# Gated linear attention inside a hybrid decoder block: the scores of two 64-token chunks as one 128x128 product, with the decay referred to the boundary between them

## The chip, the cores and the metric

The kernel runs on one NeuronCore of a Trainium2 chip. Its time is the device time of one launch, in microseconds (us): the median of several timed runs. A profiled execution, taken separately, gives the span from the first to the last instruction and the start and duration of every instruction. The engines are called by the profile's names: PE is TensorE's matmul, PEld its weight load, DVE VectorE, ACT ScalarE, POOL GpSimd, SP the engine that issues most DMAs. A matmul holds one operand still in the array (the stationary one, loaded by PEld) and streams the other past it (the moving one).

## The reference

One decoder block on 512 tokens of width 1024, all in float32: a normalized input goes through one wide projection; a gated linear attention (GLA, 4 heads, key width 128, value width 256) and a sparse attention work on its parts; their merged outputs and then a SwiGLU feed-forward are added to the residual. The change touches only the GLA. Cut to what matters (per head; `b` is the running sum of the log decay within a chunk of 64 tokens, `n` counts the 8 chunks):

```
log_a  = log_sigmoid(a_lr @ w_alpha2 + b_alpha) / 16
b      = cumsum(log_a within a chunk);  b_last = b at the chunk's last token
qe     = q * 128**-0.5 * exp(b)
ke     = k * exp(-b)
kd     = k * exp(b_last - b)
attn   = where(causal, qe @ ke.T, 0)              # inside each chunk, 64x64
o      = attn @ v + qe @ state_before_chunk
state  = exp(b_last) * state + kd.T @ v           # from chunk to chunk
```

`o` is then normalized per head and gated.

## The kernel before, in words

**Layout.** Activations are kept transposed: a tile of [128, 512] has 128 features on the partitions and the 512 tokens along the free dimension. For the GLA a head's queries `gq[h]`, keys `gk[h]` and decay sums `lam[:, h]` are such tiles (128 = the key width). The values `tok[n]` have tokens on the partitions, four tiles of 128 tokens. The kernel handles two chunks of 64 at a time, so a head has NT = 4 *pairs*, and the state is carried from pair to pair. Inside a pair the left chunk is s = 0, the right one s = 1; the helper `par` picks one side of all four pairs, a [128, 4, 64] view, 256 columns.

**Dense products.** Each of the many projections (`dense_h` with `prod`, L175 to L196) multiplies a [128 x 1024] weight block with the [1024 x 512] input. Full fp32 accuracy comes from splitting weights and input into a high and a low half in a faster format and adding three products per 128 rows (L182, L183, L184), 24 matmuls with 512 moving columns per block. The class `Stream` brings the weight blocks in: SP's DMA into `wraw` (L53, three buffers), ScalarE's conversion to `whi` (L59, two buffers), VectorE's difference `wlo` (L65, two buffers). It works one block ahead of need. `proj` (L295) evicts a finished block from PSUM with VectorE, times the token's norm factor `rb_x` (L298), or with one more scalar (L300, so far used for the sparse attention's queries).

**Order of the work.** `weave` (L78) puts a list of side steps between the dense blocks. After the blocks of gates, keys and queries, the steps of the four GLA heads are woven into the rest of the list `with_gla` (L546): for each head `gla_prep` (decay factors and products on VectorE, ScalarE and GpSimd), `gla_attn` (scores), `gla_state`, `gla_out`, `gla_end` (gate, and the split into halves at L199 and L200). The order of the steps is preparation 0, scores 0, preparation 1, state 0, output 0, scores 1, preparation 2, end 0, state 1, and so on: a head is prepared right behind the scores of the head before it. The framework adds all semaphores and orders the instructions by its own priorities; `issue_after` keeps a scan of `gla_prep` (L361) behind a given eviction, which `out_of` remembers. Each engine then works its queue in order.

**`gla_prep` (L359 to L397).** From the running sums `lam` it makes: `dd` = last minus running sum (VectorE, L371), `e1` = exp(+b) (ScalarE, L372), `e2` = exp(-b) (L373, one buffer), `dd` exponentiated in place (L374), `el` = exp(last) (L375), `dec` = the decay over a pair (L377). Then the operands. VectorE writes two blocks of `q3` [128, 4, 3, 64]: left queries times exp(b) in block 0, right queries likewise in block 2, both times the scale QSCALE (L387). GpSimd makes six products of [128 x 256]: block 1 of `q3`, the right queries carried over the left chunk (L389); `ke`, the left keys times exp(-b) (L391); `kx`, one side the right keys times exp(-b) (L392), the other the left keys times exp(last - b) (L393); `ku`, the keys for the state (L394, L395).

**`gla_attn` (L399 to L416).** For each of the four pairs two fp32 products into one PSUM bank: `ke` (64 columns, stationary) with block 0 of `q3` gives the left chunk's 64x64 scores (L404); `kx` (128 columns, stationary) with block 2 gives the scores of the right chunk's 64 queries against all 128 keys (L405). Eight masked copies on VectorE take the part on and above the diagonal into `at`, which was zeroed once (L409, L410). Three transposes of `ku` follow (L414) and ScalarE copies them out (L415). `gla_state` multiplies them with the values (L423), and `gla_out` adds the score product (L439) and, from the second pair on, blocks 0 and 1 of `q3` times the state (L441).

After the heads, the space of their tiles is used by the sparse attention, whose compression weights come by a GpSimd DMA (L583) and are read at L609.

Of the kernel before, what the change touches and what calls it, by code (L numbers as in the profile page):

```python
# [8 lines left out]
F32 = mybir.dt.float32  # L9
F32R = mybir.dt.float32r  # L10
U8 = mybir.dt.uint8
AF = mybir.ActivationFunctionType
OP = mybir.AluOpType
# [3 lines left out]
S = 512  # L17
D = 1024
KD = D // 128
NT = S // 128  # L20
# [8 lines left out]
QSCALE = 128.0 ** -0.5  # L29
# [63 lines left out]
def hybrid_block_kernel(ctx: ExitStack, tc: tile.TileContext, I, outT):  # L93
    nc = tc.nc
    act, dve, pool, pe = nc.scalar, nc.vector, nc.gpsimd, nc.tensor
# [35 lines left out]
    rb_x = base.tile([128, S], F32, name="rb_x")  # L131
# [23 lines left out]
    for key in with_gla + with_cmp + with_att + late:  # L155
        kind, n = key
# [72 lines left out]
    for k in range(KD):  # L229
        xt = xin.tile([128, S], F32, tag="xt", bufs=8, name="xt")  # L230
        nc.sync.dma_start(xt, I["xT"][k])
        if k % 2 == 0:
# [3 lines left out]
                                 in1=hT[:, k, :].bitcast(F32), op0=OP.mult, op1=OP.subtract)  # L236
# [12 lines left out]
    for g in range(3):  # L249
        pss = [bank(t) for t in tags[g]]  # L250
        for c in range(4):
            wh, wl = st.next(("tok", g, c))
            for i in range(NT):
                if (g, c, i) == (0, 3, 2):
                    ps = token_sums([acc_x], "acc")
                    rsqrt_mean(rs_x, ps[:, 0:NT], D, EPS)
                t = slice(i * 128, (i + 1) * 128)
# [7 lines left out]
        if g == 0:  # L265
            ps = over_partitions(rs_x, "acc")
# [28 lines left out]
    def proj(n, dst, scale=None):  # L295
        ps = dense_h(n)
        if scale is None:
            out_of[n] = dve.tensor_tensor(out=dst, in0=ps, in1=rb_x, op=OP.mult)  # L298
        else:
            dve.scalar_tensor_tensor(out=dst, in0=ps, scalar=scale, in1=rb_x, op0=OP.mult, op1=OP.mult)  # L300


    p_gt = tc.tile_pool(name="glat", bufs=1, reuse_waits="tile")
# [53 lines left out]
    gst = {}  # L357

    def gla_prep(h):  # L359
        with tc.issue_after(out_of[T_GK + h + 1 if h + 1 < HG else T_GQ + h].ins):  # L360
            dve.tensor_tensor_scan(out=lam[:, h], data0=keep.rearrange("p c t -> p (c t)"), data1=lam[:, h],  # L361
                                   initial=0.0, op0=OP.mult, op1=OP.add)
        bb = lam[:, h].rearrange("p (c t) -> p c t", t=64)
        last = bb[:, :, 63:64]
        T = 1.0 / 16.0
        e1 = gt.tile([128, S], F32, tag="e1", bufs=1, name="e1")
        e2 = gt.tile([128, S], F32, tag="e2", bufs=1, name="e2")
        dd = gt.tile([128, 8, 64], F32, tag="dd", bufs=2, name="dd")
        el = gt.tile([128, 8], F32, tag="el", bufs=2, name="el")
        dec = gt.tile([128, 4], F32, tag="dec", bufs=2, name="dec")  # L370
        dve.tensor_tensor(out=dd, in0=last.to_broadcast([128, 8, 64]), in1=bb, op=OP.subtract)  # L371
        act.activation(out=e1, in_=lam[:, h], func=AF.Exp, scale=T)  # L372
        act.activation(out=e2, in_=lam[:, h], func=AF.Exp, scale=-T)  # L373
        act.activation(out=dd, in_=dd, func=AF.Exp, scale=T)  # L374
        act.activation(out=el, in_=last.rearrange("p c o -> p (c o)"), func=AF.Exp, scale=T)  # L375
        el2 = el.rearrange("p (n two) -> p n two", two=2)
        dve.tensor_tensor(out=dec, in0=el2[:, :, 0], in1=el2[:, :, 1], op=OP.mult)  # L377

        def par(t, s):
            return t.rearrange("p (n two t) -> p n two t", two=2, t=64)[:, :, s, :]  # L380
        ddf = dd.rearrange("p c t -> p (c t)")
        q3 = gt.tile([128, NT, 3, 64], F32, tag="gq3", bufs=2, name="gq3")
        ke = gt.tile([128, NT, 64], F32, tag="gke", bufs=1, name="gke")
        kx = gt.tile([128, NT, 2, 64], F32, tag="gkx", bufs=1, name="gkx")
        ku = gt.tile([128, NT, 2, 64], F32, tag="gku", bufs=1, name="gku")
        for s in range(2):
            dve.scalar_tensor_tensor(out=q3[:, :, 2 * s, :], in0=par(gq[h], s), scalar=QSCALE, in1=par(e1, s),  # L387
                                     op0=OP.mult, op1=OP.mult)
        pool.tensor_tensor(out=q3[:, :, 1, :], in0=q3[:, :, 2, :],  # L389
                           in1=el2[:, :, 0:1].to_broadcast([128, NT, 64]), op=OP.mult)  # L390
        pool.tensor_tensor(out=ke, in0=par(gk[h], 0), in1=par(e2, 0), op=OP.mult)  # L391
        pool.tensor_tensor(out=kx[:, :, 1, :], in0=par(gk[h], 1), in1=par(e2, 1), op=OP.mult)  # L392
        pool.tensor_tensor(out=kx[:, :, 0, :], in0=par(gk[h], 0), in1=par(ddf, 0), op=OP.mult)  # L393
        pool.tensor_tensor(out=ku[:, :, 1, :], in0=par(gk[h], 1), in1=par(ddf, 1), op=OP.mult)  # L394
        pool.tensor_tensor(out=ku[:, :, 0, :], in0=kx[:, :, 0, :],  # L395
                           in1=el2[:, :, 1:2].to_broadcast([128, NT, 64]), op=OP.mult)
        gst[h] = [q3, ke, kx, ku, dec]  # L397

    def gla_attn(h):  # L399
        q3, ke, kx, ku, dec = gst[h]  # L400
        at = ats[h % 2]
        ps = bank("tp")
        for n in range(NT):
            pe.matmul(ps[0:64, n * 128:n * 128 + 64], ke[:, n, :], q3[:, n, 0, :], start=True, stop=True)  # L404
            pe.matmul(ps[:, n * 128 + 64:(n + 1) * 128], kx[:, n].rearrange("p s t -> p (s t)"), q3[:, n, 2, :],  # L405
                      start=True, stop=True)
        p4 = ps.rearrange("p (n c) -> p n c", c=128)
        for n in range(NT):
            dve.copy_predicated(out=at[0:64, n, 0:64], mask=triu8[0:64, 0:64], data=p4[0:64, n, 0:64])  # L409
            dve.copy_predicated(out=at[:, n, 64:128], mask=triu8[:, 64:128], data=p4[:, n, 64:128])  # L410
        ps = bank("tp")
        kut = gt.tile([128, 3, 128], F32, tag="gkut", bufs=1, name="gkut")
        for n in range(3):
            pe.transpose(ps[:, n * 128:(n + 1) * 128], ku[:, n].rearrange("p s t -> p (s t)"), ident)  # L414
        act.copy(kut.rearrange("p n d -> p (n d)"), ps[:, 0:384])  # L415
        gst[h].append(kut)  # L416

    def gla_state(h):
        q3, ke, kx, ku, dec, kut = gst[h]
        ss = gt.tile([128, 3, 256], F32, tag="gs", bufs=2, name="gs")  # L420
        for n in range(3):
            ps = bank("sc")
            pe.matmul(ps[:, 0:256], kut[:, n, :], tok[n][:, h * 256:(h + 1) * 256], start=True, stop=True)  # L423
            if n == 0:
                act.copy(ss[:, 0, :], ps[:, 0:256])
            else:
                dve.scalar_tensor_tensor(out=ss[:, n, :], in0=ss[:, n - 1, :], scalar=dec[:, n:n + 1],
                                         in1=ps[:, 0:256], op0=OP.mult, op1=OP.add)
        gst[h].append(ss)

    def gla_out(h):
        q3, ke, kx, ku, dec, kut, ss = gst[h]
        at = ats[h % 2]
        ps = [bank("acc"), bank("acc")]
        ssq = gt.tile([128, NT], F32, tag="gssq", bufs=2, name="gssq")
        o = gt.tile([128, NT, 256], F32, tag="go", bufs=1, name="go")
        for n in range(NT):
            out = ps[n // 2][:, (n % 2) * 256:(n % 2) * 256 + 256]
            pe.matmul(out, at[:, n, :], tok[n][:, h * 256:(h + 1) * 256], start=True, stop=(n == 0))  # L439
            if n > 0:  # L440
                pe.matmul(out, q3[:, n, 0:2, :].rearrange("p s t -> p (s t)"), ss[:, n - 1, :], start=False, stop=True)  # L441
            act.activation(out=o[:, n, :], in_=out, func=AF.Square, accum_out=ssq[:, n:n + 1])
        rs = gt.tile([128, NT], F32, tag="grs", bufs=2, name="grs")
        rsqrt_mean(rs, ssq, 256, EPS)
        for n in range(NT):
            out = ps[n // 2][:, (n % 2) * 256:(n % 2) * 256 + 256]
            act.activation(out=o[:, n, :], in_=out, func=AF.Copy, scale=rs[:, n:n + 1])
        gst[h] = o
# [58 lines left out]
    def run(key, ps=None):  # L507
        kind, n = key
        if kind == "pa":
            if ps is None:  # L510
                ps = bank("mm")
                prod(ps, st.next(key), lambda k: ah[:, k, :], lambda k: al[:, k, :], 0, 8, 8)
            dve.scalar_tensor_tensor(out=ta[n], in0=ta[n], scalar=1.0, in1=ps, op0=OP.add, op1=OP.mult)
        elif n >= T_MB:
            where = mid2 if n < T_MB + 4 else mixp if n < T_MB + 7 else mix2
            tb[n - T_MB] = merge_gate(n, where.tile([128, S], F32, name="tb%d" % (n - T_MB)), ps)
        elif n >= T_MA:
            ta[n - T_MA] = merge_gate(n, slot(n - T_MA), ps)
        elif n >= T_R:
            proj_r(n - T_R)  # L520
        elif n >= T_KV + 2:
            proj(n, kst["sw"[n - T_KV - 2]])
        elif n >= T_KV:
            compress_in(n)
        elif n >= T_NQ:
            proj(n, qst[n - T_NQ], 0.125)
        elif n >= T_GK:
            proj(n, gk[n - T_GK])
        else:
            proj(n, gq[n])  # L530

    def runs(keys):
        return [lambda key=key: run(key) for key in keys]
# [1095 lines left out]
```

## Time and profile before

| | |
|---|---|
| timed runs | 871.92, 872.35, 873.64 us; median 872.35 |
| profiled execution, its own time as the page gives it (the span) | 870.5 us |
| granted TensorE clock, mean over the span | 0.996 |
| instructions | 13817 |
| score products of a head (8 products, 16 passes) | 2.40 us from the first to the transposes behind them |
| scores of the four heads start at | 112.43, 142.38, 178.85, 215.34 us |
| masked copies | 16 of 64x64, median 216 ns; 16 of 128x64, median 214 ns |

The page lists for each engine the busy time and its share of the span, then the chain of work that ended last, followed back from the last instruction. The trace behind it answers by line, by wait, by stretch of time and as a timeline. In a timeline a row is start, duration, engine, line, operation, the tile written and those read, the shape, and in brackets how long the engine stood idle before it and what released it. Matmul rows show the stationary tile (rows*columns) and then the moving one (partitions x columns). Matmuls are pipelined and their ends are modelled, so what one costs in a stream is the distance between starts. An fp32 matmul appears as two passes, each with its weight load.

### The profile page before, as it was taken

The page shows a single profiled execution, that of the slowest core. Times are in us where ns is not written, and L with a number is a line of the kernel's source. Part 1 is how long each engine was busy: PE and PEld are TensorE (multiplying, and loading weights), DVE is VectorE, ACT ScalarE, POOL GpSimd, SP SyncE. Part 2 cuts the span into 40 slices and gives each one's busy share as a digit, 9 for nine tenths or more (in the row PEclk, how much of TensorE's full clock was granted, in tenths as well). Part 3 has the DMA queues.
Part 4 walks back from the last instruction along what each step waited for, and adds up shares of the span by engine and source line. Part 5 has one row for each costly group of instructions (what it writes and reads, how often), then busy time and mean ns, then how long its engine had stood idle before and what let it go on. Part 6 is the DMA issues. An engine that isn't in the chain of part 4 may idle for free.

```text
span 870.5 us, 13817 instructions
## 1 busy us (share of the span) xinstructions
PE 856.8 (98%) x5268; PEld 759.8 (87%) x5268; DVE 594.5 (68%) x1125; ACT 486.3 (56%) x862; POOL 141.5 (16%) x169
## 2 busy tenths in 40 slices
PE   9999999999999999999999999999999999999995
PEld 8998877887888788888887999899999999889995
DVE  8224753534464888887767468998778779829876
ACT  7335434333362788888744577765666656525441
POOL 1000322020030001000000354111111110001343
PEclk9999999999999999999999999999999999999998
DMA  7332221222241444545317849679877873335222
GB/s 237 97 98 93 97 83 63 79 66 74 73 152 49 120 98 103 117 98 122 85 49 226 269 137 247 125 199 233 186 171 176 195 176 85 94 87 170 86 98 98
DMA packets 36914, 111.23 MB, mean 128 GB/s; under 512 B 4236, under 2 KB 6300, under 8 KB 36720
## 3 DMA queue, kind: packets, MB, share of 16 engines
q1 hardware_dynamic: 27232, 82.49, 29.7%
q0 software_dynamic: 8896, 27.32, 16.8%
q8 instruction: 41, 0.67, 0.3%
q10 hardware_dynamic: 720, 0.54, 0.2%
q14 instruction: 25, 0.20, 0.1%
HBM read 95.66 MB, written 4.19 MB: 115 GB/s over the span
## 4 chain that ended last, share of the span: by engine, by line
PE 91%; ACT 4%; DVE 2%; issue 1%; DMA 1%; POOL 0%; SPq 0%; ACTq 0%; DVEq 0%; POOLq 0%
PE ps_mm L182 11%; PE ps_mm L184 11%; PE ps_mm L183 11%; PE ps_mm L1191 6%; PE ps_tp L1191 6%; PE ps_sc L1191 5%; PE ps_acc L1191 5%; PE ps_sc L1482 4%; PE ps_acc L1482 2%; PE ps_mm L1482 2%; PE ps_tp L792 2%; PE ps_acc L184 1%; PE ps_acc L183 1%; PE ps_acc L182 1%; PE ps_sc L182 1%; PE ps_sc L184 1%
## 5 line engine op out<-in xcount | busy, mean ns | idle before, releaser
L59 ACT CAST whi<-wraw 128x1024 fp32r<-128x1024 f32 (+2 forms) x81 | 80.1, 989 | 150.4 <-PE ps_mm L183 66.9
L182 PE MATMUL ps_mm<-hT_hi,whi 128*128 128x512 f32 x344 | 139.9, 407 | 0.0
L184 PE MATMUL ps_mm<-hT_hi,wlo 128*128 128x512 f32 x344 | 137.0, 398 | 0.0
L183 PE MATMUL ps_mm<-hT_lo,whi 128*128 128x512 f32 x344 | 136.1, 395 | 0.0
L65 DVE TENSOR_TENSOR wlo<-wraw,whi 128x1024 fp32r<-128x1024 f32 (+2 forms) x66 | 75.0, 1137 | 51.1 <-ACT whi L59 51.0
L184 PEld LDWEIGHTS ps_mm<-hT_hi,wlo 128*128 128x128 f32 x344 | 64.7, 188 | 15.4 <-DVE wlo L65 0.3
L182 PEld LDWEIGHTS ps_mm<-hT_hi,whi 128*128 128x128 f32 x344 | 64.9, 189 | 14.0
L183 PEld LDWEIGHTS ps_mm<-hT_lo,whi 128*128 128x128 f32 x344 | 64.9, 189 | 13.0
L752 ACT ACTIVATE p<-p,mx 128x512 f32<-128x512 f32 (+1 forms) x64 | 35.9, 561 | 8.8 <-DVE mx L750 7.8
L200 DVE TENSOR_TENSOR pl<-ps_tp,ph 128x512 fp32r<-128x512 f32 (+1 forms) x64 | 31.0, 489 | 13.2 <-ACT ph L199 12.5
L63 POOL DMA_DIRECT2D wlo<-wraw x15 | 13.0, 864 | 154.2 <-ACT wlo L62 154.2
L750 DVE CUSTOM_DVE_ANT_0 p<-ps_sc,causal 128x512 f32<-128x512 f32 (+1 forms) x64 | 30.2, 486 | 6.2 <-PE ps_sc L743 6.1
L1090 POOL DMA_DIRECT2D w_uu<-in_w_up x19 | 16.4, 865 | 84.6 <-PE ps_sc L1191 27.0
L199 ACT CAST ph<-ps_tp 128x512 fp32r<-128x512 f32 (+1 forms) x64 | 26.3, 415 | 4.1 <-PE ps_tp L792 3.6
L792 PE MATMUL ps_tp<-ident,p 128*128 128x128 f32 x160 | 27.7, 273 | 0.4 <-ACT pc L686 0.3
L792 PEld LDWEIGHTS ps_tp<-ident,p 128*128 128x128 f32 x160 | 20.6, 140 | 8.0 <-ACT pc L686 0.7
L182 PE MATMUL ps_mm<-gla_hi,whi 128*128 128x512 f32 x64 | 26.2, 410 | 0.0
L466 DVE TENSOR_TENSOR sr<-ps_mm,rb_x 128x512 f32<-128x512 f32 x8 | 5.5, 692 | 29.0 <-PE ps_mm L184 29.0
L184 PE MATMUL ps_mm<-gla_hi,wlo 128*128 128x512 f32 x64 | 25.3, 395 | 0.0
L183 PE MATMUL ps_mm<-gla_lo,whi 128*128 128x512 f32 x64 | 25.3, 395 | 0.0
L1106 ACT CAST w_hl<-s 128x1024 fp32r<-128x1024 f32 x12 | 12.6, 1047 | 19.6 <-issue 15.8
L1106 ACT CAST w_d1h<-s 128x1024 fp32r<-128x1024 f32 x13 | 13.7, 1051 | 17.2 <-issue 12.5
(862 smaller groups left out, 2778.2 us busy)
## 6 DMA issues: line engine op xcount, KB each, us to landing
wraw<-in_w_t SPq DMA_DIRECT2D x40, 512.0 KB, 3.5
wraw<-in_w_gate SPq DMA_DIRECT2D x21, 512.0 KB, 5.8
rw<-in_w_up SPq DMA_DIRECT2D x19, 512.0 KB, 4.2
wlo<-wraw POOLq DMA_DIRECT2D x15, 512.0 KB, 4.5
wlo<-in_w_gate POOLq DMA_DIRECT2D x13, 512.0 KB, 7.2
wraw<-in_w_tok SPq DMA_DIRECT2D x12, 440.0 KB, 4.1
w_uu<-in_w_up POOLq DMA_DIRECT2D x19, 256.0 KB, 5.8
wraw<-in_w_proj SPq DMA_DIRECT2D x8, 512.0 KB, 3.5
```

The source lines that it names most:

```text
L59: self.nc.scalar.copy(hi[:, :cols], raw[:, :cols])
L65: self.nc.vector.tensor_tensor(out=lo[:, :cols], in0=raw[:, :cols], in1=hi[:, :cols].bitcast(F32), op=OP.subtract)
L182: pe.matmul(ps[:, t], wh[:, c], xh(k)[:, t], start=(k == 0), stop=False)
L183: pe.matmul(ps[:, t], wh[:, c], xl(k)[:, t], start=False, stop=False)
L184: marks.append(pe.matmul(ps[:, t], wl[:, c], xh(k)[:, t], start=False, stop=(k == ktot - 1)))
L199: act.copy(hi, src)
L200: dve.tensor_tensor(out=lo, in0=src, in1=hi.bitcast(F32), op=OP.subtract)
L750: dve.tensor_tensor_reduce(out=o, in0=s, in1=causal[:, S - n:S], scale=-1.0, scalar=-NEG, op0=OP.add, op1=OP.min, accum_out=mx[:, i:i + 1])
L752: act.activation(out=o, in_=o, func=AF.Exp, scale=-1.0, bias=mx[:, i:i + 1], accum_out=z[:, i:i + 1])
L792: pe.transpose(tp[:, i * 128:(i + 1) * 128], p[:, OFF[i] + k * 128:OFF[i] + (k + 1) * 128], ident)
L1191: pe.matmul(o, w[:, c], x[q], start=(first and q == 0 and i == 0), stop=(q == 3 and i == 2), skip_group_check=True)
L1482: pe.matmul(o, w[:, c], x[q], start=(first and q == 0 and i == 0), stop=(q == KH - 1 and i == 2), skip_group_check=True)
```

## The change

The left queries for the scores are referred to the end of the left chunk: a new block of the query tile holds q * exp(b - last), made from a second factor, exp(-(last - b)). With the left keys in `kx`, which already carry exp(last - b), their product is exp(b_q - b_k), as before. So one stationary tile `kx` (left and right keys, 128 columns) and one moving tile (left and right queries, 128 columns) give all the scores of a pair; the quarter of right keys against left queries is masked out. `ke` goes. The query tile has four blocks now (left with exp(b), right carried over the left chunk, left referred to the boundary, right with exp(b)). `e2` is made by two exponentials, its left half from `dd` before `dd` is exponentiated, its right half from the running sums. The eight masked copies become one over the whole bank. The scale QSCALE moves from `gla_prep` to the eviction of the query projection.

```diff
-            dve.scalar_tensor_tensor(out=dst, in0=ps, scalar=scale, in1=rb_x, op0=OP.mult, op1=OP.mult)
+            out_of[n] = dve.scalar_tensor_tensor(out=dst, in0=ps, scalar=scale, in1=rb_x, op0=OP.mult,
+                                                 op1=OP.mult)
...
-        e2 = gt.tile([128, S], F32, tag="e2", bufs=1, name="e2")
+        e2 = gt.tile([128, NT, 2, 64], F32, tag="e2", bufs=1, name="e2")
...
-        act.activation(out=e2, in_=lam[:, h], func=AF.Exp, scale=-T)
+        b2 = lam[:, h].rearrange("p (n two t) -> p n two t", two=2, t=64)
+        d2 = dd.rearrange("p (n two) t -> p n two t", two=2)
+        act.activation(out=e2[:, :, 0, :], in_=d2[:, :, 0, :], func=AF.Exp, scale=-T)
+        act.activation(out=e2[:, :, 1, :], in_=b2[:, :, 1, :], func=AF.Exp, scale=-T)
...
-        q3 = gt.tile([128, NT, 3, 64], F32, tag="gq3", bufs=2, name="gq3")
-        ke = gt.tile([128, NT, 64], F32, tag="gke", bufs=1, name="gke")
+        q4 = gt.tile([128, NT, 4, 64], F32, tag="gq4", bufs=2, name="gq4")
...
-            dve.scalar_tensor_tensor(out=q3[:, :, 2 * s, :], in0=par(gq[h], s), scalar=QSCALE, in1=par(e1, s),
-                                     op0=OP.mult, op1=OP.mult)
-        pool.tensor_tensor(out=q3[:, :, 1, :], in0=q3[:, :, 2, :],
+            dve.tensor_tensor(out=q4[:, :, 3 * s, :], in0=par(gq[h], s), in1=par(e1, s), op=OP.mult)
+        pool.tensor_tensor(out=q4[:, :, 1, :], in0=q4[:, :, 3, :],
                            in1=el2[:, :, 0:1].to_broadcast([128, NT, 64]), op=OP.mult)
-        pool.tensor_tensor(out=ke, in0=par(gk[h], 0), in1=par(e2, 0), op=OP.mult)
-        pool.tensor_tensor(out=kx[:, :, 1, :], in0=par(gk[h], 1), in1=par(e2, 1), op=OP.mult)
+        pool.tensor_tensor(out=q4[:, :, 2, :], in0=par(gq[h], 0), in1=e2[:, :, 0, :], op=OP.mult)
+        pool.tensor_tensor(out=kx[:, :, 1, :], in0=par(gk[h], 1), in1=e2[:, :, 1, :], op=OP.mult)
...
         for n in range(NT):
-            pe.matmul(ps[0:64, n * 128:n * 128 + 64], ke[:, n, :], q3[:, n, 0, :], start=True, stop=True)
-            pe.matmul(ps[:, n * 128 + 64:(n + 1) * 128], kx[:, n].rearrange("p s t -> p (s t)"), q3[:, n, 2, :],
-                      start=True, stop=True)
+            pe.matmul(ps[:, n * 128:(n + 1) * 128], kx[:, n].rearrange("p s t -> p (s t)"),
+                      q4[:, n, 2:4, :].rearrange("p s t -> p (s t)"), start=True, stop=True)
         p4 = ps.rearrange("p (n c) -> p n c", c=128)
-        for n in range(NT):
-            dve.copy_predicated(out=at[0:64, n, 0:64], mask=triu8[0:64, 0:64], data=p4[0:64, n, 0:64])
-            dve.copy_predicated(out=at[:, n, 64:128], mask=triu8[:, 64:128], data=p4[:, n, 64:128])
+        dve.copy_predicated(out=at, mask=triu8.unsqueeze(1).to_broadcast([128, NT, 128]), data=p4)
...
-                pe.matmul(out, q3[:, n, 0:2, :].rearrange("p s t -> p (s t)"), ss[:, n - 1, :], start=False, stop=True)
+                pe.matmul(out, q4[:, n, 0:2, :].rearrange("p s t -> p (s t)"), ss[:, n - 1, :], start=False, stop=True)
...
-            proj(n, gq[n])
+            proj(n, gq[n], QSCALE)
```

The remaining lines of the diff only rename `q3` to `q4` where the tiles are handed on, and drop `ke` there.

More of the change, by code (lines that the diff above doesn't have):

```diff
@@ L396, in gla_prep @@
                            in1=el2[:, :, 1:2].to_broadcast([128, NT, 64]), op=OP.mult)
-        gst[h] = [q3, ke, kx, ku, dec]
+        gst[h] = [q4, kx, ku, dec]
     def gla_attn(h):
-        q3, ke, kx, ku, dec = gst[h]
+        q4, kx, ku, dec = gst[h]
         at = ats[h % 2]
@@ L418, in gla_state @@
     def gla_state(h):
-        q3, ke, kx, ku, dec, kut = gst[h]
+        q4, kx, ku, dec, kut = gst[h]
         ss = gt.tile([128, 3, 256], F32, tag="gs", bufs=2, name="gs")
@@ L431, in gla_out @@
     def gla_out(h):
-        q3, ke, kx, ku, dec, kut, ss = gst[h]
+        q4, kx, ku, dec, kut, ss = gst[h]
         at = ats[h % 2]
```

## The prediction, on record before the changed kernel ran

> **What bounds the kernel now.** I read the page first: the span, TensorE's busy line and the shares of the chain of work that ended last.
>
> ```profile
> span 870.5 us, 13817 instructions
> PE   856.8 (98%) x5268; PEld 759.8 (87%) x5268; DVE 594.5 (68%) x1125; ACT 486.3 (56%) x862; POOL 141.5 (16%) x169
> PE 91%; ACT 4%; DVE 2%; issue 1%; DMA 1%; POOL 0%; SPq 0%; ACTq 0%; DVEq 0%; POOLq 0%
> ```
>
> TensorE is busy nearly all the time and carries 91% of the chain. An average says nothing about one stage, so next I read the busy time by stretches: from just before the first head's preparation to the last head's end (84 to 250), and the two stretches behind it.
>
> ```profile
> core 0: us, PE busy (x) PEld busy (x) DVE busy (x) ACT busy (x) POOL busy (x), PEclk, DMA share, GB/s
> 84.00:250.00 166.00, 165.92 (x756) 132.47 (x755) 83.34 (x140) 66.28 (x123) 26.89 (x33) 1.00 0.24 77
> 250.00:292.00 42.00, 41.94 (x201) 34.85 (x200) 28.44 (x61) 17.74 (x36) 5.75 (x9) 1.00 0.30 95
> 292.00:362.00 70.00, 69.45 (x373) 56.52 (x372) 58.69 (x171) 61.11 (x137) 6.01 (x7) 1.00 0.48 111
> ```
>
> In the stretch that the change touches, TensorE runs 165.92 of 166 us at the full granted clock; VectorE is busy half of it, ScalarE 40%, GpSimd 16%, the DMA engines 24%. What TensorE does less there, the end should come earlier by, unless another wait takes the place. The waits of this stretch show what the others wait for:
>
> ```profile
> ACT whi L59 <- PE ps_mm L183: 47.8, 16, 5.7
> ...
> POOL gke L391 <- PE ps_tp L404: 22.0, 3, 11.4
> ...
> PEld ps_tp L404 <- issue: 1.5, 4, 0.4
> ...
> ACT e L373 <- POOL gkx L392: 0.7, 2, 0.4
> ```
>
> The weight conversion on ScalarE (L59) stood waiting for TensorE 47.8 us in all: weights are ready ahead of need. The one wait of TensorE's weight loads that belongs to the changed lines is 1.5 us over four heads, ahead of the first score product, and no engine's work ends it.
>
> **The score products, the term that counts.** TensorE around the scores of the first head, from its timeline (start, duration, line; x2 since each fp32 product is two passes):
>
> ```profile
> 112.10 0.40 PE L184 MATMUL ps_mm<-hT_hi,wlo 128*128 128x512 f32 x1
> 112.43 0.33 PE L404 MATMUL ps_tp<-gq,gke 128*64 128x64 f32 x2
> 112.69 0.43 PE L405 MATMUL ps_tp<-gq,gkx 128*128 128x64 f32 x2
> 113.05 0.33 PE L404 MATMUL ps_tp<-gq,gke 128*64 128x64 f32 x2
> ...
> 114.56 0.43 PE L405 MATMUL ps_tp<-gq,gkx 128*128 128x64 f32 x2
> 114.83 0.50 PE L414 MATMUL ps_tp<-ident,gku 128*128 128x128 f32 x3
> ...
> 215.34 0.33 PE L404 MATMUL ps_tp<-gq,gke 128*64 128x64 f32 x2
> ...
> 217.74 0.50 PE L414 MATMUL ps_tp<-ident,gku 128*128 128x128 f32 x3
> ```
>
> Ends of matmuls are modelled, so I count from start to start. A product of L404 takes 0.26 us, one of L405 0.36, the pair of them 0.62 per chunk pair; from the first of the eight to the transposes behind them are 2.40 us, in the last head (215.34 to 217.74) as in the first. From the last dense matmul (112.10) to the transposes (114.83) are 2.73 us.
>
> The new form, a 128-column stationary tile and 128 moving columns in fp32, is in the trace elsewhere, unbroken: the broadcast of the norm's factor (L220). Two neighbours bound it: the same stationary size with 64 moving columns (L659) and with 256 (L423).
>
> ```profile
> 26.83 1.05 PE L220 MATMUL ps_acc<-ident,rs_x 128*128 128x128 f32 x8
> L220 PE MATMUL ps_acc<-ident,rs_x x8: 272/276/276, 26.8 to 27.6; 128*128 128x128 f32 x8
> 274.80 3.79 PE L659 MATMUL ps_sc<-kdg,qst 128*128 128x64 f32 x32
> 126.13 0.39 PE L184 MATMUL ps_mm<-hT_hi,wlo 128*128 128x512 f32 x1
> 126.36 1.03 PE L423 MATMUL ps_sc<-tok,gkut 128*128 128x256 f32 x4
> L423 PE MATMUL ps_sc<-tok,gkut 128*128 128x256 f32 x4 | 1.0, 380 | 0.0
> ```
>
> L220: eight passes from first start to last end in 1.05, one lasting 0.276, so (1.05 - 0.276) / 7 = 0.111 us from start to start. L659: (3.79 - 0.276) / 31 = 0.113, with half the moving columns (its own pass is taken as L220's). So up to 128 moving columns a pass costs the same, 0.111. L423: (1.03 - 0.38) / 3 = 0.217 for 256 columns. A new product is then two passes, 0.223, and four of them 0.89 us. The entry from the dense stream into such a form costs nothing extra: 126.13 to 126.36 is 0.23, the dense matmuls' own spacing, while 112.10 to 112.43 is 0.33. New length from the dense matmul to the transposes: 0.23 + 0.89 = 1.12, or 1.17 if the step to the transposes keeps 0.05 of its present excess (114.56 + 0.11 for the second pass, then 114.83). Saved per head 2.73 - 1.12 = 1.61, or 1.56; for four heads 6.4 or 6.2; I take 6.3. Bounds from the neighbours: a pass can't well be cheaper than the 0.111 that L220 and L659 share, and if it cost the 0.217 of the 256-column row, a head would need 0.23 + 8 x 0.217 = 1.97, saving 0.76, 3.1 in all.
>
> Why the old pair costs 0.62 where two uniform fp32 products cost 0.45: it alternates a 64-column stationary tile with a 128-column one, and each turn costs. The Trainium skill, "TensorEngine Tiling (Array Packing)", Key Properties, says that changing the tiling mode drains the engine; the 0.26 and 0.36 against 0.22 agree with that, but no row here separates it. The forecast doesn't hang on the reason: the old cost is measured whole.
>
> **The rest of TensorE and what is moved.** Transposes (L414), state and output products keep number and form; L441 reads the first two blocks of the new tile as it did of the old.
>
> **VectorE.** Eight masked copies per head become one of 128x512 with the mask repeated.
>
> ```profile
> 115.03 0.22 DVE L409 COPY_PREDICATED at<-triu,ps_tp 64x64 f32<-64x64 uint8 x1 [0.67 <-PE ps_tp L405]
> ...
> 115.96 0.21 DVE L410 COPY_PREDICATED at<-triu,ps_tp 128x64 f32<-128x64 uint8 x1
> 116.09 1.20 DVE L65 TENSOR_TENSOR wlo<-wraw,whi 128x1024 fp32r<-128x1024 f32 x1
> 112.54 0.69 DVE L298 TENSOR_TENSOR gq<-ps_mm,rb_x 128x512 f32<-128x512 f32 x1 [2.06 <-PE ps_mm L184]
> L300 DVE SCALAR_TENSOR_TENSOR qst<-ps_mm,rb_x x4: 691/692/692, 126.6 to 170.0; 128x512 f32<-128x512 f32 x4
> ```
>
> The eight take 115.03 to 116.09, 1.06 us. The trace has no masked copy of that size; the nearest is L298, 128x512 out of PSUM, 0.69; bounds 0.21 (one narrow copy) and 1.06 (no cheaper than now). Gain 0.4 per head on an engine that is idle half the stretch: off the path. What stands queued behind it is the weights' low half (L65), which then comes earlier. The query projections get their scale inside the eviction: L298 (0.69) becomes the form of L300 (0.69), nothing; the two multiplications of 128x256 lose a scalar, nothing that matters.
>
> **ScalarE and GpSimd.** One exponential of 128x512 becomes two of 128x256, the first of which reads the difference tile before that is exponentiated in place. GpSimd's six products per head stay six: the one for the left keys goes, one for the left queries comes, of the same size.
>
> ```profile
> 112.35 1.04 ACT L59 CAST whi<-wraw 128x1024 fp32r<-128x1024 f32 x1 [1.20 <-PE ps_mm L183]
> 114.71 0.73 POOL L391 TENSOR_TENSOR gke<-gk,e 128x256 f32<-128x256 f32 x1 [11.39 <-PE ps_tp L404]
> 115.40 0.74 POOL L392 TENSOR_TENSOR gkx<-gk,e 128x256 f32<-128x256 f32 x1
> 116.17 0.63 ACT L373 ACTIVATE e<-lam 128x512 f32<-128x512 f32 x1 [0.32 <-POOL gkx L392]
> 134.33 0.38 ACT L442 ACTIVATE go<-ps_acc 128x256 f32<-128x256 f32 x1
> L393 POOL TENSOR_TENSOR gkx<-gk,dd x4: 735/834/1797, 96.7 to 182.9; 128x256 f32<-128x256 f32 x4
> ```
>
> Two of 0.38 (L442's size) against 0.63: 0.13 more per head on ScalarE, which is idle 60% of the stretch. The new wait on ScalarE holds what is queued behind it, the weight conversions (L59), whose results TensorE needs; they have the 47.8 us of waiting above as cover, and without it each microsecond would be one on the path (the slower rival below). The score product needs what GpSimd makes fourth, before and after; those four were made from 96.7 to 182.9, each more than 14 us ahead of its head's scores (the first ready by 98.5 at the latest, scores at 112.43; the last by 184.7, scores at 215.34). A second operand for it from GpSimd fits there.
>
> **What is late next.** Behind the heads, the compression's weights are loaded into the space they leave.
>
> ```profile
> 250.36 0.53 POOL L583 DMA_DIRECT2D cw<-in_cmp_w  x1 [2.11 <-DVE gla_lo L200]
> DMA to landing us min/median/max: 8.1/8.1/8.1
> L609 PEld LDWEIGHTS ps_sc<-ct,cw x32: 189/206/208, 263.6 to 270.4; 128*128 128x128 f32 x32
> ```
>
> They land at about 258.5 and are first read at 263.6: 5 us to spare, and the load is released by the last head's end, which moves with TensorE. So is the rest: TensorE is idle 0.06 us from 250 to 292 and 0.55 in the stretch behind. I expect the whole saving at the end.
>
> **Sum.** Profiled span 870.5 - 6.3 = 864.2. The runs' median, 872.35, is 1.85 above the span, and the runs spread from 871.92 to 873.64, so about 0.2% (1.75 us) is what can be told from no change. Forecast: 872.35 - 6.3 = 866.0.
>
> **The rivals.**
>
> Wide price: the new passes cost like the 256-column row. For it: none of the 128-column rows has dense data on both sides (L220 multiplies by the identity). Against: L423 has dense data and costs per column the same. Time 872.35 - 3.1 = 869.3.
>
> Only the load counts: the passes follow the columns loaded, 0.111 for 128 and half, 0.056, for 64, so the old pair's share is 0.33, and the 0.29 above it belongs to something that stays (the operands, the shared bank). Then 0.111 goes per pair, 16 x 0.111 = 1.8, to 870.6, at the edge of what can be told. Beside it the Trainium skill, "TensorE: Matmul & The Clock Gate", LDWEIGHTS (loading the stationary operand), gives a load time in proportion to the columns; L220's spacing agrees for 128, and L404's 0.26 for two loads of 64 does not. Against: L659 has the same bank, fp32 and 64 moving columns, and no excess.
>
> Lost behind: something that doesn't move with TensorE sets a later stage, and the time stays 872.4. For it: from 292 to 362 ScalarE and VectorE are busy 61 and 59 of 70 us. Against: their work starts from TensorE's, and TensorE waits for almost nothing there.
>
> Slower: ScalarE's new order. The second factor tile has one buffer, so the next head's exponential waits for GpSimd's read of it (L392), and that for the scores (22.0 us of such waits on GpSimd); the difference's exponential, free to run ahead so far, now queues behind. If the schedule puts these ahead of a conversion that the next dense block needs, that block starts after GpSimd's product (115.40 + 0.74, 1.3 after the scores' end at 114.83), two exponentials (0.76), the conversion (1.04) and the low half (1.20): 4.3 us late, for the two heads whose exponential waits like this (0.7 us, 2 times) 8.6, against 6.3 saved: 872.35 + 2.3 = 874.7. It decides from 3.2 us per head. Against: now that wait costs 0.7 us in all, and the conversions run one block ahead of need.
>
> **How the numbers follow.** Chances: forecast 0.78, wide price 0.05, load only 0.05 (half faster, half same), lost behind 0.07, slower 0.05. Faster 0.78 + 0.05 + 0.03 = 0.86, same 0.02 + 0.07 = 0.09, slower 0.05. Range: up to the wide price, 869.3; down to 864.2, the forecast less 1.3 for the upper spread of the runs (873.64 against 872.35) and 0.5 for shorter waits on VectorE's queue.
>
> **What would show it.** In the changed profile: one score group, 128*128 128x128, 32 passes spaced 0.11; 1.1 us from the last dense matmul to the transposes; the stretch of the heads shorter by 6.3 with TensorE still full; four masked copies near 0.7. Spacing of 0.2 means the wide price; 0.4 to 0.5 per product, the load-only rival; TensorE waiting for a conversion or its low half behind the scores, the slower one; a head stretch shorter by 6 and an equal end, the lost gain.

## The result, and the profile after

The changed kernel took 866.2 us (median of 4 runs, 865.91 to 866.61) against 872.13 for the kernel before in the same comparison (4 runs, 871.91 to 873.64), 5.9 us less: ratio 0.9931, 95% interval 0.9918 to 0.9944, which is 4.9 to 7.2 us. The forecast was 866.0 with a range of 864.2 to 869.3. The profiled span went from 870.5 to 864.1 us, 6.4 less; the sum had 6.3.

From the changed kernel's page, the span, the busy time and the chain by engine:

```profile
span 864.1 us, 13723 instructions
PE 850.6 (98%) x5236; PEld 755.6 (87%) x5236; DVE 595.7 (69%) x1097; ACT 486.2 (56%) x866; POOL 145.6 (17%) x169
PE 90%; ACT 4%; DVE 2%; issue 2%; DMA 1%; POOL 0%; SPq 0%; ACTq 0%; DVEq 0%; POOLq 0%
```

TensorE's busy time fell by 6.2 us (856.8 to 850.6), nearly what the span lost; the totals of VectorE, ScalarE and GpSimd stayed or rose. This is TensorE's timeline around the first head's scores and the last head's, in the changed kernel (start, duration, line):

```profile
111.96 0.40 PE L184 MATMUL ps_mm<-hT_hi,wlo 128*128 128x512 f32 x1
112.19 1.05 PE L406 MATMUL ps_tp<-gq,gkx 128*128 128x128 f32 x8
113.08 0.49 PE L413 MATMUL ps_tp<-ident,gku 128*128 128x128 f32 x3
...
210.02 0.39 PE L184 MATMUL ps_mm<-hT_hi,wlo 128*128 128x512 f32 x1
210.25 1.05 PE L406 MATMUL ps_tp<-gq,gkx 128*128 128x128 f32 x8
211.14 0.49 PE L413 MATMUL ps_tp<-ident,gku 128*128 128x128 f32 x3
```

From the last dense matmul to the transposes are 1.12 us in the first head (111.96 to 113.08) and in the last; before, 2.73. Eight passes stand where sixteen stood. One lasts 0.275, so they are (1.05 - 0.275) / 7 = 0.111 us apart.

Since TensorE sets the pace, the span can be cut at two of its own marks: the last dense matmul ahead of the first head's scores, and the transposes behind the last head's. The kernel before had 112.10 ahead, 105.64 between (217.74 - 112.10) and 652.76 behind; the changed one 111.96, 99.18 and 652.96. The whole difference, 6.46 us, lies between the marks, and 4 x (2.73 - 1.12) = 6.44 of it is the score groups. The stages behind them gave nothing back and took nothing that can be told: in the nine traces of this record, that part lasts from 652.06 to 653.40 us.

The other engines' rows on the changed lines:

```profile
L390 DVE TENSOR_TENSOR gq<-gq,e 128x256 f32<-128x256 f32 x8 | 5.2, 689 | 1.8 <-PE ps_acc L440 1.8
L393 POOL TENSOR_TENSOR gq<-gq,e 128x256 f32<-128x256 f32 x4 | 3.7, 926 | 42.3 <-PE ps_acc L440 42.2
L409 DVE COPY_PREDICATED at<-triu,ps_tp 128x512 f32<-128x512 uint8 x4 | 2.9, 727 | 0.0
L376 ACT ACTIVATE e<-dd 128x256 f32<-128x256 f32 x4 | 1.7, 418 | 5.1 <-POOL gkx L394 3.4 <-DVE dd L372 1.7
L377 ACT ACTIVATE e<-lam 128x256 f32<-128x256 f32 x4 | 1.6, 410 | 0.0
```

Columns behind the count: busy us in all, mean ns of one, idle time ahead of it and what ended that. One masked copy takes 0.73 us in place of eight in 1.06. The two half exponentials take 0.83, not 0.63, and ScalarE now stands 5.1 us in all ahead of the one that reads `dd`. VectorE's query products (L390) went from a median of 0.42 us to one of 0.69. None of this reaches TensorE. Its matmuls have no row of waits from 84 to 250 us, before or after. Of its weight loads' rows the 1.5 us ahead of the score products are gone, and two others stay as they were (2.1 and 1.3 us, both for ScalarE's evictions):

```profile
PEld ps_acc L438 <- ACT go L441: 2.1, 7, 0.4
...
PEld ps_sc L422 <- ACT gs L424: 1.3, 4, 0.3
```

### The profile page after: what moved, and what is told of

It is laid out like the page before. It is cut to its first block, busy times and chain, and to the rows that moved or that the text cites. A ratio compares the mean times of both kernels' runs of the same rounds, so it can differ in the third digit from the quotient of the medians.

```text
span 864.1 us, 13723 instructions
## 1 busy us (share of the span) xinstructions
PE 850.6 (98%) x5236; PEld 755.6 (87%) x5236; DVE 595.7 (69%) x1097; ACT 486.2 (56%) x866; POOL 145.6 (17%) x169
## 4 chain that ended last, share of the span: by engine, by line
PE 90%; ACT 4%; DVE 2%; issue 2%; DMA 1%; POOL 0%; SPq 0%; ACTq 0%; DVEq 0%; POOLq 0%
PE ps_mm L182 11%; PE ps_mm L184 11%; PE ps_mm L183 11%; PE ps_mm L1190 6%; PE ps_tp L1190 6%; PE ps_sc L1190 5%; PE ps_acc L1190 5%; PE ps_sc L1481 4%; PE ps_acc L1481 2%; PE ps_mm L1481 2%; PE ps_tp L791 2%; PE ps_acc L184 1%; PE ps_acc L182 1%; PE ps_acc L183 1%; PE ps_sc L183 1%
## 5 line engine op out<-in xcount | busy, mean ns | idle before, releaser
L65 DVE TENSOR_TENSOR wlo<-wraw,whi 128x1024 fp32r<-128x1024 f32 (+2 forms) x66 | 75.6, 1145 | 50.7 <-ACT whi L59 50.5
```

The source lines that it names most:

```text
L65: self.nc.vector.tensor_tensor(out=lo[:, :cols], in0=raw[:, :cols], in1=hi[:, :cols].bitcast(F32), op=OP.subtract)
```

## The experiments

Each ran beside the kernel before on the same chip; in the first four's group that took 873.0 us, in the others' 872.18. The changed kernel was not in these groups, so times are set against its 866.2 only roughly, and the ratios and the traces decide.

**1. The narrow products grouped.** This is the kernel before, with its two kinds of product in two loops:

```diff
         for n in range(NT):
             pe.matmul(ps[0:64, n * 128:n * 128 + 64], ke[:, n, :], q3[:, n, 0, :], start=True, stop=True)
+        for n in range(NT):
             pe.matmul(ps[:, n * 128 + 64:(n + 1) * 128], kx[:, n].rearrange("p s t -> p (s t)"), q3[:, n, 2, :],
                       start=True, stop=True)
```

> The kernel before with one edit: the four left products (64 stationary columns) first, then the four right ones (128 columns), instead of alternating. Same products, same operands, same results. Theory (each turn between a 64-column and a 128-column stationary tile costs): six of the eight turns go. The eight passes of the right products then run 0.11 us apart as in the uniform rows, the eight of the left ones at most 0.11 apart; from the last dense matmul to the transposes 0.33 + at most 0.9 + about 0.1 + 0.9, so 1.9 to 2.3 us instead of 2.73; the time 1.8 to 3.4 us below the kernel before, about 870. Rival (the excess belongs to the operands or the bank, not to the turns): 2.73 us as before and no change in time.

It took 868.92 us (868.43 to 869.53), ratio 0.9956 (0.9943 to 0.9968). TensorE's timeline of this kernel, first head:

```profile
112.29 0.40 PE L184 MATMUL ps_mm<-hT_hi,wlo 128*128 128x512 f32 x1
112.61 0.68 PE L404 MATMUL ps_tp<-gq,gke 128*64 128x64 f32 x8
113.22 1.10 PE L406 MATMUL ps_tp<-gq,gkx 128*128 128x64 f32 x8
114.16 0.50 PE L415 MATMUL ps_tp<-ident,gku 128*128 128x128 f32 x3
```

The same sixteen passes take 1.87 us from the dense matmul to the transposes (112.29 to 114.16) instead of 2.73. By themselves the narrow passes are (0.68 - 0.222) / 7 = 0.065 apart, the wide ones (1.10 - 0.275) / 7 = 0.118, where 0.222 and 0.275 are the lengths of one. Only the order changed, so 0.86 us per head, 3.4 in all, was the price of the six turns between the two stationary widths that are gone, about 0.14 each. The rival, by which nothing would change, fell. Two turns are left: the step from the dense matmul is 0.32, not 0.23, and the narrow group takes 0.61, not 8 x 0.065 = 0.52.

The gain came out above the range that was expected (1.8 to 3.4 us; the median fell by 4.1, the profiled span by 3.9). Between the marks the trace has 102.25 us (112.29 to 214.54), 3.39 less than before. The rest is no effect of the scores: behind the marks this execution took 652.06 us, 0.70 less than the kernel before's, within the spread of that part in traces whose work there is the same on TensorE.

**2. Uniform, but in halves.** This is the changed kernel, with each product split over its moving columns:

```diff
-            pe.matmul(ps[:, n * 128:(n + 1) * 128], kx[:, n].rearrange("p s t -> p (s t)"),
-                      q4[:, n, 2:4, :].rearrange("p s t -> p (s t)"), start=True, stop=True)
+            for s in range(2):
+                pe.matmul(ps[:, n * 128 + s * 64:n * 128 + (s + 1) * 64], kx[:, n].rearrange("p s t -> p (s t)"),
+                          q4[:, n, 2 + s, :], start=True, stop=True)
```

> The changed kernel with each 128x128 product issued as two with the same stationary tile and 64 moving columns each; same results. Theory (passes with up to 128 moving columns cost 0.11 whatever their width, no turns since all stationary tiles have 128 columns, and TensorE's time in this stretch is the kernel's): 16 passes per head 0.113 apart, 0.23 + 1.81 = 2.04 us from the last dense matmul to the transposes instead of 1.12, so 0.9 per head and 3.7 in all above the changed kernel, about 869.9, still 2.3 below the kernel before. Rival (cost follows the moving columns): the same 1.1 us and no change from the changed kernel, 866.2. Rival (the excess belongs to many small products as such): 2.4 to 2.7 us and the time of the kernel before, 872.

It took 870.08 us (868.74 to 870.76), ratio 0.9965 (0.9952 to 0.9977). The first head's timeline:

```profile
112.19 0.39 PE L184 MATMUL ps_mm<-hT_hi,wlo 128*128 128x512 f32 x1
112.42 1.89 PE L407 MATMUL ps_tp<-gq,gkx 128*128 128x64 f32 x16
114.15 0.50 PE L414 MATMUL ps_tp<-ident,gku 128*128 128x128 f32 x3
```

The sixteen passes of 64 moving columns are (1.89 - 0.275) / 15 = 0.108 apart, as dear as those of 128. They take 1.96 us instead of 1.12 (2.04 were expected). Between the marks are 102.52 us (112.19 to 214.71), 3.34 more than in the changed kernel, and 4 x 0.84 = 3.36. So half the moving columns bring nothing once every pass loads 128 stationary columns, and half as many of them saves 0.84 us per head. The rival by which cost follows the moving columns fell, and so did the one by which many small products are dear as such (2.4 to 2.7 us).

**3. Eight copies again.** This is the changed kernel with the kernel before's masked copies:

```diff
-        dve.copy_predicated(out=at, mask=triu8.unsqueeze(1).to_broadcast([128, NT, 128]), data=p4)
+        for n in range(NT):
+            dve.copy_predicated(out=at[0:64, n, 0:64], mask=triu8[0:64, 0:64], data=p4[0:64, n, 0:64])
+            dve.copy_predicated(out=at[:, n, 64:128], mask=triu8[:, 64:128], data=p4[:, n, 64:128])
```

> The changed kernel with the eight masked copies of the kernel before instead of one. Theory (all of the gain is TensorE's): VectorE 0.3 us longer per head off the path, the time that of the changed kernel, 866.2 within 0.5. Rival (the shorter queue on VectorE brings part of the gain): up to 4 x 0.3 = 1.3 us slower, 867.5.

It took 866.46 us (865.7 to 867.07), ratio 0.9926 (0.9914 to 0.9938), that of the changed kernel. The masked copies carry no part of the gain that can be told; the rival's upper value, 867.5, lies above all five runs. Between the marks its trace has the changed kernel's 99.18 us (112.12 to 211.30), and so have those of experiments 4 and 5.

**4. The instruction form of the query products.** This is the changed kernel with the old form on VectorE:

```diff
-            dve.tensor_tensor(out=q4[:, :, 3 * s, :], in0=par(gq[h], s), in1=par(e1, s), op=OP.mult)
+            dve.scalar_tensor_tensor(out=q4[:, :, 3 * s, :], in0=par(gq[h], s), scalar=1.0, in1=par(e1, s),
+                                     op0=OP.mult, op1=OP.mult)
```

> The changed kernel with VectorE's two query products per head written with a scalar of 1.0 (scalar_tensor_tensor), the instruction form of the kernel before, instead of tensor_tensor. Their pair lasts 1.3 us in all four heads of the changed kernel against 0.76 in three of four before. Theory (they slow down because a GpSimd product now starts beside them): still 1.3 us. Rival (the instruction form costs it): 0.76. Both: the time stays 866.2 within 0.5, since VectorE is off the path.

It took 865.63 us (865.52 to 866.47), ratio 0.9921 (0.9907 to 0.9934), not to be told from the changed kernel. A later head in this kernel's timeline, and the eight products (min/median/max in ns):

```profile
135.35 1.31 DVE L390 SCALAR_TENSOR_TENSOR gq<-gq,e 128x256 f32<-128x256 f32 x2 [0.62 <-PE ps_acc L441]
135.46 0.91 POOL L394 TENSOR_TENSOR gq<-gq,e 128x256 f32<-128x256 f32 x1 [17.51 <-PE ps_acc L441]
...
L390 DVE SCALAR_TENSOR_TENSOR gq<-gq,e x8: 411/690/965, 95.6 to 170.5; 128x256 f32<-128x256 f32 x8
```

The pair still takes 1.31 us: the form isn't it. Both engines start within 0.11 us of each other, since both waited for the same matmul (L441) to free the query tile.

**5. No GpSimd product beside them.** This is the changed kernel with the new product moved to VectorE:

```diff
-        pool.tensor_tensor(out=q4[:, :, 2, :], in0=par(gq[h], 0), in1=e2[:, :, 0, :], op=OP.mult)
+        dve.tensor_tensor(out=q4[:, :, 2, :], in0=par(gq[h], 0), in1=e2[:, :, 0, :], op=OP.mult)
```

> The changed kernel with the new product (left queries times the boundary factor) on VectorE instead of GpSimd; same results. Theory (the two query products last 1.3 us because a GpSimd product runs beside them): without that neighbour VectorE's products of this form take about 0.4 us each in the later heads, three in 1.2. Rival (the new four-block layout slows them): 0.65 to 0.7 each, three in 2. Time in both: 866.2 within 0.7, since neither engine is on the path.

It took 865.42 us (865.02 to 866.3), ratio 0.9925 (0.9911 to 0.9938), again the changed kernel's time. VectorE's products in this kernel, by line, and a later head in its timeline:

```profile
L390 DVE TENSOR_TENSOR gq<-gq,e 128x256 f32<-128x256 f32 x8 | 3.0, 417 | 1.8 <-PE ps_acc L440 1.8
...
L393 DVE TENSOR_TENSOR gq<-gq,e 128x256 f32<-128x256 f32 x4 | 1.7, 414 | 0.0
...
135.86 0.42 DVE L393 TENSOR_TENSOR gq<-gq,e 128x256 f32<-128x256 f32 x1
136.04 0.72 POOL L391 TENSOR_TENSOR gq<-gq,el 128x256 f32<-128x256 f32 x1 [18.34 <-DVE grs L213]
```

They take 0.41 to 0.42 each, in the same layout: it was the neighbour. Not every GpSimd product does it, though. The last two rows show one (L391, whose second operand is a repeated column) that starts 0.18 us into VectorE's third product; that still takes 0.42, and GpSimd's takes 0.72 where it took 0.62 in the changed kernel. Why they differ is open. The time is the changed kernel's, so this version does not beat it.

**6. ScalarE loaded.** This is the changed kernel with one exponential issued nine times:

```diff
-        act.activation(out=e1, in_=lam[:, h], func=AF.Exp, scale=T)
+        for _ in range(9):
+            act.activation(out=e1, in_=lam[:, h], func=AF.Exp, scale=T)
```

> The changed kernel with the exponential of the left factor (128x512, 0.63 us) issued nine times instead of once per head, each time with the same result: 5 us more per head on ScalarE, 20 us in all, more than three times what the change saves. Theory (ScalarE's conversions run a block ahead of need and its waits are covered): at most 1 us longer than the changed kernel, 866.2 to 867.2, and TensorE waits for no conversion in the heads' stretch. Rival (the cover is thin, as the slower case of the prediction had it): conversions come late behind the repeated exponentials, TensorE stands for 1 us or more per head, 870 or above.

It took 865.53 us (864.91 to 867.43), ratio 0.9927 (0.9914 to 0.9939): no longer than the changed kernel. The load is 17 us rather than the 20 of the expectation: ScalarE's busy time from 84 to 250 us, the fourth pair of columns, went from 70.15 (changed kernel) to 87.53, so 4.3 us per head. The waits in this kernel, and the stretch of the heads, in the changed kernel first:

```profile
ACT whi L59 <- PE ps_mm L183: 45.1, 15, 5.7
...
DVE wlo L65 <- ACT whi L59: 10.1, 18, 2.1
```

```profile
84.00:250.00 166.00, 165.92 (x752) 133.95 (x751) 90.87 (x121) 70.15 (x134) 35.58 (x41) 1.00 0.26 86
84.00:250.00 166.00, 165.92 (x752) 133.92 (x751) 88.44 (x121) 87.53 (x164) 32.86 (x40) 1.00 0.28 86
```

Conversions are late for VectorE's low halves (10.1 us of such waits, 2.6 in the changed kernel), but the conversions themselves still wait 45.1 us for TensorE, which stays at 165.92 of 166. The thin cover of the slower rival isn't there. The profiled execution, 867.43, is the longest of the five; its first scores come at 113.78 where the changed kernel's come at 112.19. The load did not do that: TensorE is that late already 10 us into the span, where it waits 0.9 us for the input's high half (L234) among others, and the repeated exponentials begin at 95.2. Between the marks it has 99.17 us, the changed kernel's length.

**7. The turns put back.** This is the changed kernel with a narrow product ahead of each wide one:

```diff
+            pe.matmul(ps[0:64, n * 128:n * 128 + 64], kx[:, n, 0, :], q4[:, n, 2, :], start=True, stop=True)
             pe.matmul(ps[:, n * 128:(n + 1) * 128], kx[:, n].rearrange("p s t -> p (s t)"),
```

> The changed kernel with a narrow product put back ahead of each wide one: the left keys alone (64 stationary columns) times the left queries, into the left 64x64 part of the bank, which the wide product then overwrites; same results. 16 narrow products come back, and with them the turns. Theory (turns cost): 0.26 for the narrow one and 0.14 more for the wide one behind it, 0.40 per pair, 1.6 per head, 6.4 in all: the kernel before's time, 872.5, and 0.62 per pair in the trace. Rival (only the load of the columns costs): two loads of 0.065, 0.13 per pair, 2.1 in all, 868.3, and 0.35 per pair.

It took 873.74 us (11 runs, 873.07 to 874.42), ratio 1.0016 (1.0007 to 1.0025): all of the gain is gone, and 1.6 us more. The first head's timeline:

```profile
112.55 0.40 PE L184 MATMUL ps_mm<-hT_hi,wlo 128*128 128x512 f32 x1
112.88 0.33 PE L406 MATMUL ps_tp<-gq,gkx 128*64 128x64 f32 x2
113.13 0.49 PE L407 MATMUL ps_tp<-gq,gkx 128*128 128x128 f32 x2
113.55 0.33 PE L406 MATMUL ps_tp<-gq,gkx 128*64 128x64 f32 x2
...
115.49 0.49 PE L414 MATMUL ps_tp<-ident,gku 128*128 128x128 f32 x3
```

A pair takes 0.67 us (112.88 to 113.55), a head 2.94, against 1.12 without the narrow products: 1.82 per head, 7.3 in all, and between the marks 106.50 us (112.55 to 219.05) against 99.18. Two narrow passes that are worth 0.13 in a row of their kind cost 0.45 per pair when they alternate. The rival, 0.35 per pair, fell. The theory held and was low by 0.05 per pair: the wide product behind a narrow one takes 0.42 us with 128 moving columns (113.13 to 113.55) where the kernel before's, with 64, took 0.36.

## Why the prediction was right

**Score products.** The largest term was read from a row of the same form elsewhere in the trace, L220, and it came out to the hundredth: passes 0.111 apart, entry 0.23, 1.12 us per head. The 0.05 that the step to the transposes might have kept did not stay, so the upper of the two savings, 6.4, is what the profile shows, and the 6.3 was a middle. That the median came within 0.2 us of the forecast is in part luck, since the kernel before's runs spread over 1.7. Experiment 1 splits the saving: 3.4 us for the six turns that grouping takes out and 3.0 for the rest (1.87 to 1.12 per head). By its spacings that rest is an estimated 0.18 per head for the two turns left (0.09 and 0.09) and 0.57 for the passes (0.52 + 0.94 in the grouped kernel, 0.89 now). The prediction had measured the old cost whole and so did not need this split; it was right not to build on it.

**Load only.** This rival took 0.056 for a narrow pass, close to the 0.065 of experiment 1, and was wrong in what it made of the remainder: the 0.29 per pair did not belong to something that stays. The L659 row, held against it for having the same bank, writes `ps_sc`, not the scores' `ps_tp`; experiment 2 has the same passes in the scores' bank, without excess. By the Trainium skill, "TensorE: Matmul & The Clock Gate", LDWEIGHTS, load time goes by the columns; with like next to like the trace agrees roughly (0.065 for 64, 0.108 to 0.118 for 128). The Trainium skill, "TensorEngine Tiling (Array Packing)", Key Properties, has the engine drained at a change of mode; experiments 1 and 7 agree in that each change of width costs. That a drain is what happens there was argued, not shown; that the turns cost is shown. The 0.06 by which experiment 7's wide products are longer is open too: they have 64 more moving columns, and they also overwrite what the narrow ones wrote.

**Wide price** (0.217 per pass) fell with the score rows of the new profile, 0.111.

**Lost behind.** This rival fell: the 652.76 us behind the marks became 652.96. The compression's weights, named as what is late next, were sent for at 243.8, landed 7.9 us later and were first read at 257.0 (L608): 5.3 us to spare, 5.1 before.

**ScalarE, the slower rival.** The new wait came at the place named: 3.4 us in all for GpSimd's read where 0.7 had been, and 1.7 for the difference, for which the exponential in place had waited 2.6 before. The first of these is not the change's alone, since experiment 1's kernel, without the second factor, has 4.6 there. VectorE's waits for conversions stayed at 2.6 us (2.7 before). The rival needed 3.2 us per head beyond the scores in two heads to decide, and experiment 6 shows that 4.3 us more work in each head does not get there.

**Mis-sized, off the path.** Two half exponentials were put at 0.38 each from a square of that size; they take 0.42 and 0.41, so 0.20 more per head, not 0.13. The masked copy was put at 0.69 and took 0.73. The query products were said to change by "nothing that matters": per pair they went from 0.76 to 1.30 us in three heads, because the new GpSimd product starts beside them (in the first head they took 1.30 before as well, beside L392). The six GpSimd products were said to keep their size, while the new one takes 0.91 against 0.73 for the one that it replaced, and the one for the right keys 1.50 against 0.74 (medians). The latter now falls beside VectorE's scan (L362) or low halves (L65); that these are the reason was not tested. It did not count, since VectorE was busy half the stretch; on a kernel bound by VectorE this step could have been the error.

## What to carry to other kernels

Count small matmuls by the distance between starts, not by their columns: in fp32 a pass with 128 stationary columns cost 0.11 us here whether 64 or 128 columns moved past it, so two half-empty products should be one full one. Keep stationary widths alike next to each other: where masking allows it, a wider product with wasted entries beats a narrow one between wide ones, and grouping alone, with no change to the mathematics, was worth more than half of this gain. Where one engine is full and hardly waits, as here, the work taken from it is the time taken from the kernel; check it by cutting the span at that engine's own marks.

## What the runs showed of the hardware that was not expected

VectorE's fp32 products of two SBUF operands, 128x256, take 0.41 to 0.42 us alone and as a pair 1.30 when GpSimd's product of two such operands starts within 0.11 us, whichever of the two instruction forms is used (experiments 4 and 5); the GpSimd product takes 0.91 then, where its like took 0.73. Beside GpSimd's product with a repeated column (L391, experiment 5) VectorE's kept 0.42. The Trainium skill, "GPSIMD Engine Reference", Specifications, names the interface that the two share and contention with VectorE instructions of two SBUF inputs; the runs agree for the first kind of neighbour and give the price.
